# First layer's output projection: the first column pair with a quarter in seven products

## The chip, the cores and the metric

The kernel runs on one core of one Trainium2 chip. The metric is device time in microseconds (us), the median over runs. The profile is of one execution. The engines are TensorE (PE, matmuls, and PEld, its weight loads), VectorE (DVE), ScalarE (ACT), GpSimd (POOL) and SyncE (SP), whose queue issues most loads.

## The reference

A trunk of two layers over 256 tokens and a width of 2048, in float32. The part that matters is the end of the mixer in layer 0:

```
ya = head_rmsnorm(hgrn2(...), a_norm) * silu(za)        # 1024 columns
yb = rg_lru(...) * silu(zb)                             # 1024 columns
y = concatenate([ya, yb])                               # 256 x 2048
h = h + y @ e_w_out                                     # the output projection: 2048 x 2048
pl = rmsnorm(p @ ple_w, ple_norm)
h = h + sigmoid(h @ ple_gate_w) * pl                    # the gate
```

## The kernel before

**Exact products.** Each float32 operand is split into a high part (a cast to float32r) and a low part (the rest). A product is three matmuls: high x high, high x low, low x high. A weight tile of 128x1024 is loaded into the ring `raw` (5 buffers), ACT casts it into `whi`, DVE subtracts into `wlo` (4 buffers each); lines 137 and 138, or 221 and 222 in `split_weights`. An activation tile (tag `ahl`, a ring of 12 in the pool `ap`) holds both parts of 256 inputs for all tokens.

**Quarters.** A projection to 2048 columns has four chunks of 512 columns and four quarters `kq` of 512 inputs. `quarter_tok` (and `plain`, in the other path) loads the two tiles of one quarter of one chunk and does 24 matmuls of 128x128 by 512: two halves of the tokens (`hf`), four blocks of inputs, three matmuls each. `ready(act, lane)` gives `before(kq)`, which drives the lane that makes the activations of that quarter until they are in the program.

**Two chunks as a pair.** `project_two` does chunks 0 and 1 quarter by quarter in the order (0,0) (0,1) (1,0) (1,1) (0,2) (1,2) (0,3) (1,3), into two banks of the PSUM ring `pm` (tag mm) and two of `px` (tag mx).

**Seven products.** `seven` does a pair of chunks with one quarter (kq = 0) by the scheme with seven block products in place of eight. The blocks of the weights are X (chunk 0, side 0), Y (chunk 1, side 1), W (chunk 1, side 0) and Z (chunk 0, side 1); sums of them are formed on DVE (`add`, line 310) and combinations of the activations come from `combos` (tiles q4, two of them, names 1 to 4). Each product is six matmuls of 512 columns (`product`, line 235). Four banks take part: E from `px`, and A, F and B from `pm`. X and Y live in tiles from `room` (tile ch); W and Z come through the ring. `part()` gives two half-tiles, b5 and g (tile pr), which keep products 5 and 6. The string `order` writes out the order by hand: a and b are the next quarter of chunk 0 and 1, digits are products, A and F hand out chunk 0's two halves, a dot lets background lanes advance. At the end E + g (line 318) and B are handed out as chunk 1's halves. `two_and_seven` does the first pair with `project_two` and the second with `seven`, on the combinations that the first pair's time has made. In layer 1's gate (`gates`) the first pair goes through `seven` with the order `LATE` and a quarter of chunk 2 ahead of Y (`third`).

**What is around it.** While the last input projection runs, the inputs y are made: `feature_major` makes y[0] to y[3] and `gated_mix` y[4] to y[7] (line 1048 multiplies by the recurrence's output tt). Each goes tokens to features by DVE transposes (line 699) and a hop through DRAM on POOL's queue (lines 686, 689), 6 steps of the pump after its start. `out_proj` adds each half that is handed out to the residual hq (line 604), transposes it and starts the next hop.

**Pools.** The pool `m0` holds the mixer's tiles (tags f, q, k of two buffers each, and smaller ones); tt lies in tag k. The pool `e0` is opened when m0 is closed and takes the same memory: pr, two tiles ch, gr, wg (set to zero by POOL, line 1141), q4 and row. It serves the second pair of the output projection and the gate. `mixed` closes m0 when the first half of the first pair is handed out:

```
            if (c, hf) == (0, 0):
                m0_scope.close()
                pe0.append(l0.enter_context(tc.tile_pool(name="e0", bufs=1)))
```

The framework orders the instructions of each engine ahead of time, by priorities, and puts in the waits.

Of the kernel before, what the change touches and what calls it, by code (L numbers as in the profile page):

```python
# [19 lines left out]
P = 128  # L20
# [2 lines left out]
KT = D // P  # L23
EPS = 1e-6
RSQRT_MAGIC = 0x5F3759DF
ORDERS = {1: "a5a6.2aA7b.4F.bb", 2: "a5.2aA64.7F.bb"}
LATE = "a526.a7b4aAF.bb"


_PRM = [  # L30
# [15 lines left out]
def trunk(ctx: ExitStack, tc: tile.TileContext, a, out):  # L46
# [113 lines left out]
    def tokens(x, k, hf):  # L160
        return x[:, k, hf * P:(hf + 1) * P]

    def project_tok(w, j, act, before=None, begun=None):

        ps = begun or [pm.tile([P, 512], F32, name="mm", tag="mm") for _ in range(2)]
        for kq in range(1 if begun else 0, 4):
            if before is not None:
                before(kq)
            quarter_tok(w, j, kq, act, ps)
        return ps  # L170
# [13 lines left out]
        for j in range(2, n):  # L184
            yield project_tok(w, j, act)

    def two_and_seven(w, act, before, where, places, home=None, begin=None):

        qs = {}
        start("combos", combos(act, 0, qs, *where))  # L190
        for c, ps in enumerate(project_two(w, act, before)):
            for hf in range(2):
                yield c, hf, ps[hf]
        drain("combos")
        if begin is not None:
            begin()
        for b, hf, src in seven(w, 2, act, qs, (0,), *places(), home and home()):
            yield 2 + b, hf, src
# [42 lines left out]
    def plain(w, j, kq, act, ps, first=(False, False), end=False):  # L241

        parts = load_weights(w[4 * j + kq])
        for hf in range(2):
            product(ps[hf], stationary(act, (2 * kq, 2 * kq + 1), hf), parts, first[hf], end)
            if hf == 0:
                pump()

    def combos(act, kq, qs, pool, tag, bufs=None, offset=0):

        def whole(j):
            x = tp.tile([P, 512], F32, name="xr", tag="hn", bufs=3).rearrange("p (k t) -> p k t", k=2)
            v.tensor_tensor(out=x, in0=act[2 * kq + j][0], in1=act[2 * kq + j][1], op=ALU.add)
            return x[:, :, 0:P], x[:, :, P:T]

        def less(out, x, y):
            with tc.high_priority(offset=offset):
                v.tensor_tensor(out=out, in0=x, in1=y, op=ALU.subtract)

        def pair():  # L260
            c = tp.tile([P, 512], F32, name="qc", tag="th")
            return c, [c[:, i * T:(i + 1) * T].rearrange("p (k t) -> p k t", k=2) for i in range(2)]

        def keep(c, names):
            q = pool.tile([P, 1024], F32R, name="q4", tag=tag, bufs=bufs)
            with tc.high_priority(offset=offset):
                s.copy(q[:, 0:512], c)
                v.tensor_tensor(out=q[:, 512:1024], in0=c, in1=q[:, 0:512].bitcast(F32), op=ALU.subtract)
            for n, name in enumerate(names):
                qs[name, kq] = [[q[:, i * 512 + n * T + k * P:i * 512 + n * T + (k + 1) * P] for k in range(2)]  # L270
                                for i in range(2)]

        while 2 * kq + 1 not in act:
            yield
        a11, a21 = whole(0)
        a12, a22 = whole(1)
        c, (c3, c1) = pair()
        less(c3, a21, a11)
        less(c1, a21, a22)
        keep(c, (3, 1))  # L280
        yield
        d, (c2, c4) = pair()
        less(c2, a11, c1)
        less(c4, a12, c2)
        keep(d, (2, 4))
        yield

    def seven(w, j, act, qs, kqs, room, part, home=None, order=None, acc=None, before=None, third=None):

        def src(b, side, kq):  # L290
            return block(w[4 * (j + b) + kq], side * 1024, 1024)

        def load(tile_of, b, side):
            tiles = []
            for kq in kqs:
                t = tile_of()
                last["sp"] = sy.dma_start(out=t, in_=src(b, side, kq)).ins
                tiles.append(t)
            return tiles

        def ring():
            return wp.tile([P, 1024], F32, name="raw", tag="raw", bufs=5)

        def split(tiles):
            return [split_weights(t) for t in tiles]

        def add(x, y):
            with tc.high_priority(offset=400):
                for xi, yi in zip(x, y):
                    v.tensor_tensor(out=xi, in0=xi, in1=yi, op=ALU.add)  # L310

        def add_loaded(x):
            for xi, kq in zip(x, kqs):
                gp.dma_start(out=xi, in_=src(1, 0, kq), accum_op=ALU.add)

        def soon(out, in0, in1, op):
            with tc.high_priority(offset=450):
                v.tensor_tensor(out=out, in0=in0, in1=in1, op=op)

        def keep(out, bank):  # L320
            with tc.high_priority(offset=450):
                s.copy(out, bank)

        def quadrant(side, hf):
            return stationary(act, [2 * kq + side for kq in kqs], hf)

        def combo(n):
            return [[t for kq in kqs for t in qs[n, kq][x]] for x in range(2)]

        if acc is None:  # L330
            acc = len(kqs) == 2
        rest = [kq for kq in range(4) if kq not in kqs]
        E = px.tile([P, 512], F32, name="mx", tag="mx")
        A, F, B = (pm.tile([P, 512], F32, name="mm", tag="mm") for _ in range(3))
        b5, g = part(), part()
        rows = [list(rest), list(rest)]
        X = load(room, 0, 0)
        product(A, quadrant(0, 0), split(X), True)
        if acc:
            add_loaded(X)  # L340
        with tc.high_priority(offset=450):
            if home is not None:
                with tc.issue_after(last["act"]):
                    s.copy(E, home)
            s.copy(F, A)
            s.activation(B, F, AF.Copy, scale=-1.0)
        if third is not None:
            plain(w, j + 2, kqs[0], act, third, (True, True))
        Y = load(room, 1, 1)
        product(E, combo(4), split(Y), home is None)  # L350
        W = X
        if not acc:
            W = load(ring, 1, 0)
            add(Y, W)
            add(W, X)
        did = set()
        for op in order or ORDERS[len(kqs)]:
            if op in "ab":
                b = "ab".index(op)
                kq = rows[b].pop(0)  # L360
                if before is not None:
                    before(kq)
                plain(w, j + b, kq, act, ((A, F), (E, B))[b], end=not rows[b])
            elif op == "5":
                product(B, combo(1), split(W))
                add(X, Y)
                if acc:
                    add_loaded(Y)
                keep(b5, B)
            elif op == "6":  # L370
                product(B, combo(2), split(X))
                keep(g, B)
            elif op == "2":
                Z = load(ring, 0, 1)
                product(A, quadrant(1, 0), split(Z))
            elif op == "4":
                product(F, quadrant(1, 1), split(X))
            elif op == "7":
                product(B, combo(3), split(Y))
                soon(b5, B, b5, ALU.subtract)  # L380
            elif op == ".":
                pump()
            elif op == "A":
                yield 0, 0, A
            elif op == "F":
                soon(b5, F, b5, ALU.subtract)
                yield 0, 1, b5
            did.add(op)
            if op in "26" and {"2", "6"} <= did:
                add(X, Z)  # L390
        if home is None:
            soon(g, E, g, ALU.add)
            yield 1, 0, g
        else:
            soon(home, E, g, ALU.add)
            yield 1, 0, None
        yield 1, 1, B
# [377 lines left out]
    if True:  # L775
# [311 lines left out]
        for g in range(2):  # L1087
            held[g] = hp.tile([P, 2, 512], F32, name="u", tag="h")
            gate_tok(a["ez"], g, acth, held[g])
            combine()  # L1090
        for g in range(2):
            ps = project_tok(ew, 6 + g, acth)
            u = hp.tile([P, 2, 512], F32, name="u", tag="h")
# [21 lines left out]
        load_hq(i, last["hop"])  # L1115

    def mixed():
        for c, hf, src in two_and_seven(a["eo"], y, ready(y, "fm"), (ap, "ahl"), in_e0):
            if hf == 0 and c in (1, 2):
                load_hq(c + 1, last["hop"])  # L1120
            if (c, hf) == (0, 0):
                m0_scope.close()
                pe0.append(l0.enter_context(tc.tile_pool(name="e0", bufs=1)))
            yield c, hf, src

    def pieces(tile):
        return iter([tile[:, 0:512], tile[:, 512:1024]]).__next__
# [65 lines left out]
    with tc.tile_pool(name="m1", bufs=2) as m1:  # L1193
# [341 lines left out]
        def gates():  # L1535
            third = [pst.tile([P, 512], F32, name="st", tag="st") for _ in range(2)]
            before = ready(act, "fo")
            yield from seven(a["g1"], 0, act, qs1, (0,), *in_m1(), order=LATE, before=before, third=third)
            for hf, ps in enumerate(project_tok(a["g1"], 2, act, None, third)):
                yield 2, hf, ps  # L1540

        for g, hf, src in gates():
# [194 lines left out]
```

## Time and profile before

| | |
|---|---|
| median of 3 runs | 1020.06 us (1020.04 to 1020.19) |
| the profiled execution: time, span | 1020.23 us, 1018.4 us |
| mean granted clock of PE | 0.998 |
| busy: PE, DVE, ACT, POOL | 1009.4, 842.8, 661.4, 101.3 us |
| moved by DMA | 242.66 MB, 238 GB/s on average |
| first pair of the output projection | 300.17 to 343.69 us |
| second pair | 343.69 to 385.85 us |

Times inside the span count from its start. A matmul's row gives about 0.39 us because neighbours overlap in the pipeline; the spacing of starts is what adds up. Lines such as L235 are lines of the kernel before, and a line can be that of a helper.

### The profile page before, as it was taken

Reading aid. Unit: us, or ns where it says so; the run is one execution under the profiler, and the core shown is the slowest. Engines: PE = TensorE matmul, PEld = TensorE weight load, DVE = VectorE, ACT = ScalarE, POOL = GpSimd, SP = SyncE. Lnnn points to the kernel's source line nnn. Section 1 sums busy time; section 2 is a strip of 40 time slices with the busy share of each in tenths; the row PEclk is TensorE's granted clock in tenths of the full one; section 3 lists DMA queues with packets and bytes.
Section 4 is the critical chain, followed back from the end, with each engine's and each line's share of the span. In section 5 each row is a group of like instructions: output and inputs, shape, how many; then the busy total and the mean of one; then the engine's idle time right before and its main releaser. Section 6 shows DMA issues by size and latency. Waiting matters only on the chain.

```text
span 1018.4 us, 14515 instructions
## 1 busy us (share of the span) xinstructions
PE 1009.4 (99%) x5158; PEld 838.1 (82%) x5158; DVE 842.8 (83%) x1234; ACT 661.4 (65%) x949; POOL 101.3 (10%) x182
## 2 busy tenths in 40 slices
PE   9999999999999999999999999999999999999996
PEld 8888888888888888888888888888888888888886
DVE  7858969969687887898669997888889997999794
ACT  7675554686875554666557877776676777466562
POOL 0111101011111112021011100000011110102000
PEclk9999999999999999999999999999999999999999
DMA  9987756567778799487798757567879889696852
GB/s 364 330 233 240 225 177 197 166 204 225 251 235 305 238 315 291 155 284 249 258 337 250 228 166 227 166 208 201 256 193 283 233 249 356 181 288 217 279 186 83
DMA packets 69816, 242.66 MB, mean 238 GB/s; under 512 B 9040, under 2 KB 10448, under 8 KB 69744
## 3 DMA queue, kind: packets, MB, share of 16 engines
q1 hardware_dynamic: 56016, 198.08, 58.7%
q0 software_dynamic: 13296, 43.13, 16.1%
q8 instruction: 40, 0.66, 0.3%
q10 hardware_dynamic: 432, 0.52, 0.1%
q14 instruction: 32, 0.26, 0.1%
HBM read 221.78 MB, written 19.92 MB: 237 GB/s over the span
## 4 chain that ended last, share of the span: by engine, by line
PE 99%; ACT 0%; DMA 0%; issue 0%; DVE 0%; ACTq 0%; POOLq 0%
PE mm L235 29%; PE mm L211 14%; PE mm L212 14%; PE mm L213 14%; PE mx L235 8%; PE mx L211 3%; PE mx L212 3%; PE mx L213 3%; PE mm L517 1%; PE nu L1349 1%; PE mx L517 1%; PE mm L1562 1%; PE mm L1561 1%; PE mm L1563 1%; PE st L213 1%; PE st L235 1%
## 5 line engine op out<-in xcount | busy, mean ns | idle before, releaser
L137 ACT CAST whi<-raw 128x1024 fp32r<-128x1024 f32 (+1 forms) x309 | 322.6, 1047 | 211.3 <-PE mm L213 95.2
L138 DVE TENSOR_TENSOR wlo<-raw,whi 128x1024 fp32r<-128x1024 f32 (+1 forms) x309 | 371.6, 1213 | 104.0 <-ACT whi L137 97.8
L211 PE MATMUL mm<-whi,ahl 128*128 128x512 f32 x640 | 250.5, 392 | 0.0
L212 PE MATMUL mm<-wlo,ahl 128*128 128x512 f32 x640 | 249.4, 390 | 0.0
L213 PE MATMUL mm<-whi,ahl 128*128 128x512 f32 x640 | 249.3, 389 | 0.0
L235 PE MATMUL mm<-whi,ahl 128*128 128x512 f32 x720 | 231.8, 390 | 0.0
L235 PEld LDWEIGHTS mm<-whi,ahl 128*128 128x128 f32 x720 | 135.2, 188 | 27.9
L211 PEld LDWEIGHTS mm<-whi,ahl 128*128 128x128 f32 x640 | 120.2, 188 | 25.5 <-issue 0.4
L213 PEld LDWEIGHTS mm<-whi,ahl 128*128 128x128 f32 x640 | 120.2, 188 | 25.1
L235 PE MATMUL mm<-wlo,ahl 128*128 128x512 f32 x360 | 140.5, 390 | 0.0
L212 PEld LDWEIGHTS mm<-wlo,ahl 128*128 128x128 f32 x640 | 120.2, 188 | 24.3
L222 DVE TENSOR_TENSOR wlo<-ch,whi 128x1024 fp32r<-128x1024 f32 x67 | 81.1, 1221 | 12.5 <-ACT whi L221 11.1
L221 ACT CAST whi<-ch 128x1024 fp32r<-128x1024 f32 x67 | 70.1, 1050 | 26.8 <-PE mm L235 13.8
L235 PEld LDWEIGHTS mm<-wlo,ahl 128*128 128x128 f32 x360 | 67.6, 188 | 14.1 <-DVE wlo L222 0.3
L235 PE MATMUL mx<-whi,ahl 128*128 128x512 f32 x192 | 63.3, 390 | 0.0
L212 PE MATMUL mx<-wlo,ahl 128*128 128x512 f32 x128 | 49.8, 389 | 0.0
L213 PE MATMUL mx<-whi,ahl 128*128 128x512 f32 x128 | 49.8, 389 | 0.0
L211 PE MATMUL mx<-whi,ahl 128*128 128x512 f32 x128 | 49.8, 389 | 0.0
L235 PE MATMUL mm<-whi,q 128*128 128x512 f32 x144 | 49.1, 391 | 0.0
L235 PEld LDWEIGHTS mx<-whi,ahl 128*128 128x128 f32 x192 | 36.1, 188 | 7.9 <-ACT xr L575 0.4
L235 PE MATMUL mx<-wlo,ahl 128*128 128x512 f32 x96 | 37.4, 390 | 0.0
L235 PEld LDWEIGHTS mm<-whi,q 128*128 128x128 f32 x144 | 27.0, 188 | 5.7
(389 smaller groups left out, 1318.5 us busy)
## 6 DMA issues: line engine op xcount, KB each, us to landing
raw<-in_ew_dram SPq DMA_DIRECT2D x64, 512.0 KB, 5.2
raw<-in_g_dram SPq DMA_DIRECT2D x60, 512.0 KB, 4.5
raw<-in_oqk_dram SPq DMA_DIRECT2D x32, 512.0 KB, 5.5
raw<-in_eo_dram SPq DMA_DIRECT2D x30, 512.0 KB, 5.1
raw<-in_oo_dram SPq DMA_DIRECT2D x30, 512.0 KB, 6.4
raw<-in_ov_dram SPq DMA_DIRECT2D x29, 512.0 KB, 4.2
raw<-in_oog_dram SPq DMA_DIRECT2D x24, 512.0 KB, 4.1
raw<-in_oz_dram SPq DMA_DIRECT2D x20, 512.0 KB, 5.1
```

The source lines that it names most:

```text
L137: last["act"] = s.copy(h, r).ins
L138: last["dve"] = v.tensor_tensor(out=l, in0=r, in1=h.bitcast(F32), op=ALU.subtract).ins
L211: te.matmul(ps[hf], xh, wh, start=(k == 0), stop=False, skip_group_check=True)
L212: te.matmul(ps[hf], xh, wl, start=False, stop=False, skip_group_check=True)
L213: last["pe"] = te.matmul(ps[hf], xl, wh, start=False, stop=(k == KT - 1), skip_group_check=True).ins
L221: last["act"] = s.copy(hi, r).ins
L222: last["dve"] = v.tensor_tensor(out=lo, in0=r, in1=hi.bitcast(F32), op=ALU.subtract).ins
L235: last["pe"] = te.matmul(o, x, y, start=(first and k + i == 0), stop=(end and k == n - 1 and i == 2), skip_group_check=True).ins
L517: last["pe"] = te.matmul(ps[hf][:, o:o + w_], tokens(pact[x], k, hf), (hi, lo)[y][:, k * 512 + o:k * 512 + o + w_], start=(n == mine[0]), ...
L1349: te.matmul(ps[:, 0:n], x[:, i, o:o + P], y[:, b, i], start=(b == 0 and x is sh and y is vh), stop=(b == hf and y is vl))
L1561: te.matmul(o, xh, wh, start=(k == 0), stop=False)
L1562: te.matmul(o, xh, wl, start=False, stop=False)
```

## The change

The first pair of the output projection goes through `seven` as well.

- `two_and_seven` gets `first` and `qs`; the first pair then runs `seven(w, 0, ...)` with the order "3a5a6.27ba4AF.bb". Sums of weights are made on DVE, as in the second pair.
- `combos` for it is started ahead of the last two chunks of the input projection, and its two tiles serve both pairs.
- X and Y of the first pair lie in the ring of the activations (tag ahl); b5 and g lie in a tile of m0, in the slots of tag q.
- The bank A of that pair comes from `px`, not `pm`.
- m0 is closed and e0 opened (`in_m0_end`) after the first pair, no longer at its first half.
- In `seven`, Y's product and the sums behind it become the step "3" of the order, and a third chunk's quarter the steps "c" and "d"; the other orders name them so that their sequence stays as it was.
- The function `moved` is new and is not called.

```diff
-ORDERS = {1: "a5a6.2aA7b.4F.bb", 2: "a5.2aA64.7F.bb"}
-LATE = "a526.a7b4aAF.bb"
+ORDERS = {1: "3a5a6.2aA7b.4F.bb", 2: "3a5.2aA64.7F.bb"}
+LATE = "c3a526.a7b4aAF.bb"
...
-    def two_and_seven(w, act, before, where, places, home=None, begin=None):
-
-        qs = {}
-        start("combos", combos(act, 0, qs, *where))
-        for c, ps in enumerate(project_two(w, act, before)):
-            for hf in range(2):
-                yield c, hf, ps[hf]
+    def two_and_seven(w, act, before, where, places, home=None, begin=None, first=None, qs=None):
+
+        if first is not None:
+            drain("combos")
+            yield from seven(w, 0, act, qs, (0,), *first(), order="3a5a6.27ba4AF.bb", before=before, first=px)
+        else:
+            qs = {}
+            start("combos", combos(act, 0, qs, *where))
+            for c, ps in enumerate(project_two(w, act, before)):
+                for hf in range(2):
+                    yield c, hf, ps[hf]
         drain("combos")
         if begin is not None:
             begin()
...
-        A, F, B = (pm.tile([P, 512], F32, name="mm", tag="mm") for _ in range(3))
+        A, F, B = (p.tile([P, 512], F32, name=n, tag=n)
+                   for p, n in ((first, "mm" if first is pm else "mx"), (pm, "mm"), (pm, "mm")))
...
-        if third is not None:
-            plain(w, j + 2, kqs[0], act, third, (True, True))
-        Y = load(room, 1, 1)
-        product(E, combo(4), split(Y), home is None)
-        W = X
-        if not acc:
-            W = load(ring, 1, 0)
-            add(Y, W)
-            add(W, X)
...
+            if op in "cd":
+                plain(w, j + 2, "cd".index(op), act, third, (op == "c",) * 2)
+            elif op == "3":
+                Y = load(room, 1, 1)
+                product(E, combo(4), split(Y), home is None)
+                W = X
+                if not acc:
+                    W = load(ring, 1, 0)
+                    add(Y, W)
+                    add(W, X)
...
+        qsy = {}
+        start("combos", combos(y, 0, qsy, ap, "ahl"))
         for g in range(2):
             ps = project_tok(ew, 6 + g, acth)
...
-        for c, hf, src in two_and_seven(a["eo"], y, ready(y, "fm"), (ap, "ahl"), in_e0):
+        for c, hf, src in two_and_seven(a["eo"], y, ready(y, "fm"), None, in_e0, None, in_m0_end, in_m0, qsy):
             if hf == 0 and c in (1, 2):
                 load_hq(c + 1, last["hop"])
-            if (c, hf) == (0, 0):
-                m0_scope.close()
-                pe0.append(l0.enter_context(tc.tile_pool(name="e0", bufs=1)))
             yield c, hf, src
+
+    def in_m0():
+        return (lambda: ap.tile([P, 1024], F32, name="ch", tag="ahl"),
+                pieces(m0.tile([P, 1536], F32, name="pr", tag="q")[:, 0:1024]))
+
+    def in_m0_end():
+        m0_scope.close()
+        pe0.append(l0.enter_context(tc.tile_pool(name="e0", bufs=1)))
```

More of the change, by code (lines that the diff above doesn't have):

```diff
@@ L161, in tokens, with project_tok @@
         return x[:, k, hf * P:(hf + 1) * P]
-    def project_tok(w, j, act, before=None, begun=None):
+    def project_tok(w, j, act, before=None, begun=None, done=0):
         ps = begun or [pm.tile([P, 512], F32, name="mm", tag="mm") for _ in range(2)]
-        for kq in range(1 if begun else 0, 4):
+        for kq in range(done, 4):
             if before is not None:
@@ L247, in plain, with moved, known @@
                 pump()
+    def moved(qs, kq, pool, tag):
+        for q, names in qs["tiles", kq]:
+            t = pool.tile([P, 1024], F32R, name="q4", tag=tag)
+            s.copy(t, q.bitcast(F32))
+            known(qs, kq, t, names)
+            yield
+    def known(qs, kq, q, names):
+        for n, name in enumerate(names):
+            qs[name, kq] = [[q[:, i * 512 + n * T + k * P:i * 512 + n * T + (k + 1) * P] for k in range(2)]
+                            for i in range(2)]
     def combos(act, kq, qs, pool, tag, bufs=None, offset=0):
@@ L268, in keep @@
                 v.tensor_tensor(out=q[:, 512:1024], in0=c, in1=q[:, 0:512].bitcast(F32), op=ALU.subtract)
-            for n, name in enumerate(names):
-                qs[name, kq] = [[q[:, i * 512 + n * T + k * P:i * 512 + n * T + (k + 1) * P] for k in range(2)]
-                                for i in range(2)]
+            known(qs, kq, q, names)
+            qs.setdefault(("tiles", kq), []).append((q, names))
         while 2 * kq + 1 not in act:
@@ L286, in combos, with seven @@
         yield
-    def seven(w, j, act, qs, kqs, room, part, home=None, order=None, acc=None, before=None, third=None):
+    def seven(w, j, act, qs, kqs, room, part, home=None, order=None, acc=None, before=None, third=None, first=pm):
         def src(b, side, kq):
@@ L346, in seven @@
             s.activation(B, F, AF.Copy, scale=-1.0)
-        if third is not None:
-            plain(w, j + 2, kqs[0], act, third, (True, True))
-        Y = load(room, 1, 1)
-        product(E, combo(4), split(Y), home is None)
-        W = X
-        if not acc:
-            W = load(ring, 1, 0)
-            add(Y, W)
-            add(W, X)
         did = set()
         for op in order or ORDERS[len(kqs)]:
-            if op in "ab":
+            if op in "cd":
[8 more added lines that the diff above has]
+                    add(W, X)
+            elif op in "ab":
                 b = "ab".index(op)
@@ L1538, in gates @@
             yield from seven(a["g1"], 0, act, qs1, (0,), *in_m1(), order=LATE, before=before, third=third)
-            for hf, ps in enumerate(project_tok(a["g1"], 2, act, None, third)):
+            for hf, ps in enumerate(project_tok(a["g1"], 2, act, None, third, 1)):
                 yield 2, hf, ps
```

## The prediction

> **What bounds the kernel now.** I read the page's busy time first, then its chain, then TensorE's waits, then the stretches that the change touches.
>
> ```profile
> PE 1009.4 (99%) x5158; PEld 838.1 (82%) x5158; DVE 842.8 (83%) x1234; ACT 661.4 (65%) x949; POOL 101.3 (10%) x182
> PE 99%; ACT 0%; DMA 0%; issue 0%; DVE 0%; ACTq 0%; POOLq 0%
> ```
>
> TensorE (PE) is busy all the time, and the chain that ended last is all PE. The view of PE's waits has one row:
>
> ```profile
> PE st L99 <- PEq L1728: 0.8, 1, 0.8
> ```
>
> That wait is at the start, so between the first and the last matmul PE waits for nothing. A matmul taken away is worth its spacing; a wait put anywhere into PE's stream is lost in full. Now the two column pairs of the first output projection, by the windows view and the chain in order of time:
>
> ```profile
> 300.17:343.69 43.52, 43.52 (x194) 36.05 (x193) 32.66 (x40) 21.26 (x24) 5.25 (x9) 1.00 0.76 258
> 343.69:385.85 42.16, 42.16 (x188) 34.92 (x187) 37.16 (x46) 24.01 (x31) 8.98 (x16) 1.00 0.91 301
> ...
> 343.69 1.36 PE mm L235 x6
> 345.06 1.36 PE mx L235 x6
> ```
>
> Columns: length, then busy time (instructions) of PE, weight loads, DVE, ACT, POOL, and the clock, 1.00. Pair one now takes eight quarters of 24 matmuls (192) in 43.52 us; pair two is already of the changed form, 7 products of 6 and 6 quarters of 24 (186), in 42.16 us. A product is six matmuls and 1.36 us; each matmul costs 0.227 us.
>
> **The change, step by step.**
>
> *Matmuls.* Pair one gets pair two's count: 192 - 186 = 6 fewer, 43.52 - 42.16 = 1.36 us gained, so it would end at 342.33. This is 0.13% of the kernel, and nothing else in the change can give more.
>
> *DVE and ACT.* 19 weight splits instead of 16, four sums of 128x1024, three corrections of 128x512; the combinations move ahead.
>
> ```profile
> L138 DVE TENSOR_TENSOR wlo<-raw,whi 128x1024 fp32r<-128x1024 f32 x14 | 17.1, 1221 | 9.5 <-ACT whi L137 9.0
> L310 DVE TENSOR_TENSOR raw<-raw,ch 128x1024 f32<-128x1024 f32 x1 | 1.2, 1210 | 0.0
> L318 DVE TENSOR_TENSOR pr<-mm,pr 128x512 f32<-128x512 f32 x2 | 1.4, 684 | 0.0
> ...
> 263.10 0.69 DVE L152 TENSOR_TENSOR ahl<-xr,ahl 128x512 fp32r<-128x512 f32 x1 [0.37 <-ACT ahl L151]
> 268.37 2.36 DVE L138 TENSOR_TENSOR wlo<-raw,whi 128x1024 fp32r<-128x1024 f32 x2 [4.58 <-ACT whi L137]
> 297.00 1.29 DVE L253 TENSOR_TENSOR xr<-ahl 128x512 f32<-128x512 f32 x2
> 313.74 0.69 DVE L268 TENSOR_TENSOR q<-qc,q 128x512 fp32r<-128x512 f32 x1
> ```
>
> DVE gains 3 x 1.22 + 4 x 1.21 + 3 x 0.68 = 10.5 us here and ACT three casts. The combinations (now from 297.00 to 314.4) can run as soon as y's first two tiles are there, at 263.8, where DVE next idles 4.58 us; their q is then ready long before the second product asks at 301.5. Pair two does the same set of work within 37.16 us of DVE in its 42.16, and PE never waits there. I cost it at nothing; the cover is DVE's remaining 5 us.
>
> *Order of y.* The new order reaches quarter 2 after three products and one quarter: 300.17 + 3 x 1.36 + 5.44 = 309.7 (its second tile 1.36 later, 311.1), and quarter 3 after six products and three quarters, at 324.7. Before they were due four and six quarters in, 321.9 and 332.8. From the timelines of DVE and POOL and the view of the tile dzb:
>
> ```profile
> 306.52 0.68 DVE L1048 TENSOR_TENSOR xr<-r,tt 128x512 f32<-128x512 f32 x1
> 312.00 0.68 DVE L152 TENSOR_TENSOR ahl<-xr,ahl 128x512 fp32r<-128x512 f32 x1
> 324.20 1.29 DVE L1048 TENSOR_TENSOR xr<-r,tt 128x512 f32<-128x512 f32 x2
> 325.58 1.29 DVE L152 TENSOR_TENSOR ahl<-xr,ahl 128x512 fp32r<-128x512 f32 x2
> ...
> 287.09 2.18 POOL L689 DMA_DIRECT2D r<-dzb  x4 [4.16 <-ACT xr L717]
> 309.15 2.18 POOL L689 DMA_DIRECT2D r<-dzb  x4 [3.99 <-DMA dzb<-w]
> DMA to landing us min/median/max: 4.2/5.5/7.4
> ```
>
> With the old times quarter 2's second tile is ready at 312.7, 1.6 us late, and quarter 3's at 326.9, 0.8 us after its own due time (324.7 + 1.36). Both can move up: the transposed data are in after the fourth issue, 289.3 and 311.3, plus about 5.5 us. DVE loses the combinations from this stretch, so I take 0; the ends are 0 and 1.6 us.
>
> *Pair one's chain tiles and banks.* X and Y take slots of the activations' ring that the last input projection frees every 5.44 us, so X is loaded by about 295; A lies in the other PSUM ring and needs no bank of that projection. The same 16 loads of 512 KB go through SP's queue. Nothing.
>
> *The pool.* This step decides. The two half-tiles b5 and g now lie in a tile of m0 (`in_m0`), so m0 closes only after pair one has been handed out, and e0 opens after that. e0 holds X and Y of pair **two**.
>
> ```profile
> 287.15 2.29 DVE L1038 TENSOR_TENSOR_SCAN tt<-av,it 128x1024 f32<-128x1024 f32 x1
> 325.56 0.81 SPq L297 DMA_DIRECT2D ch<-in_eo_dram  x2
> 325.61 0.52 POOL L1141 MEMSET wg<- 128x512 f32 x1 [12.85 <-ACT ahl L151]
> SPq L297 <- DVE xr L1048: 0.9, 1, 0.9
> ```
>
> (Timelines of DVE, SP and POOL, and SP's waits.) Both e0 tiles, X's load on SP and wg's memset on POOL, start within 0.1 us of the end of the last L1048 (324.20 + 1.29 = 325.49), the last instruction that reads a tile of m0 (tt). SP's own waits name it. By the sizes in the code X lies where m0 kept f and later av, which the scan at 287.15 was the last to touch; so I read that the hold is for the whole pool, not for the overlapping tile. It costs nothing before: 18 us remain until X's product at 343.69. After the change the last reader of m0 is the addition of g to hq, behind pair one's last quarter. Pair two shows how long that takes, and the view of the tile ch what a load into it and its split take:
>
> ```profile
> 383.28 0.68 DVE L318 TENSOR_TENSOR pr<-mx,pr 128x512 f32<-128x512 f32 x1
> 383.88 0.68 DVE L253 TENSOR_TENSOR xr<-ahl 128x512 f32<-128x512 f32 x1
> 384.48 0.69 DVE L604 TENSOR_TENSOR hq<-pr,hq 128x512 f32<-128x512 f32 x1
> ...
> DMA to landing us min/median/max: 4.4/5.2/6.0
> 336.93 1.05 ACT L221 CAST whi<-ch 128x1024 fp32r<-128x1024 f32 x1 [2.71 <-PE mm L213]
> 338.01 1.23 DVE L222 TENSOR_TENSOR wlo<-ch,whi 128x1024 fp32r<-128x1024 f32 x1 [1.00 <-ACT whi L221]
> ```
>
> E is complete 12 matmuls before the pair's end (385.85 - 2.72 = 383.13) and g is read by 385.17, 2.04 us later. In the changed pair one: 342.33 - 2.72 + 2.04 = 341.65, and X is issued 0.07 later, at 341.72. The two loads into ch landed after 4.4 and 6.0 us; I take X 4.4 (346.12) and Y, issued 0.43 later, 6.0 (348.15). Cast and split end 2.31 after the cast's start: X's low part at 348.5, Y's at 350.5. The second of six matmuls needs the low part, so Y's product ends 5 x 0.227 later, at 351.6, against 342.33 + 2.72 = 345.05 without a wait: 6.6 us lost. The ends of this term: no operation between the two on DVE (0.6 us less) and 3.4 us for both landings, the least that the loads into raw took, give 4.3; one more split of 1.22 ahead of the addition and 1.6 us more per landing give 9.4. The view of the tile raw, from 310 to 350:
>
> ```profile
> DMA to landing us min/median/max: 3.4/4.9/8.5
> ```
>
> Behind X on SP wait Y and later raw loads; the first raw tiles of pair two go ahead as slots are free. On POOL the memset, 0.52 us, waits too; the hop of columns 0 would lie before it. Nothing later absorbs the loss, since PE has no other slack.
>
> The Trainium skill (DMA: Bandwidth & Descriptors, section Anatomy of one DMA) fits a transfer on the gpsimd path as 2.0 us plus the bytes at 436 GB/s, as an estimate 3.2 us for 512 KB; with that for both landings the term would be 4.7 us and the total 1.9 us lower. The rows above, 4.4 and 6.0 on SP, are longer, so the sum does not go by it.
>
> *The clock.* PE would stand from 342.5 to X's first matmul at 347.2, 4.7 us. What a pause does is seen only at the kernel's end:
>
> ```profile
> 1010.04 0.28 PE L1563 MATMUL mm<-whi,ahl 128*128 128x256 f32 x1
> 1013.00:1014.00 1.00, 0.00 (x0) 0.00 (x0) 1.00 (x4) 0.72 (x1) 0.00 (x0) 0.69 0.00 0
> ...
> 0.78 3.75 PE L99 MATMUL st<-const-float32-1.0 128*128 128x128 f32 x16 [0.78 <-PEq L1728]
> 4.18 3.40 PE L517 MATMUL mx<-whi,ahl 128*128 128x256 f32 x12
> 7.42 1.08 PE L517 MATMUL mx<-wlo,ahl 128*128 128x512 f32 x4
> ```
>
> PE ends at 1010.32; the slice from 1013 to 1014 has a granted clock of 0.69, which is half clock for its last 0.62 us, from 1013.38, 3.06 us after. So 4.7 us is enough. At the start PE works from 0.78 and is at full pace by 7.42 at the latest: at most 6.6 us at half pace, 3.3 us lost. The other end is 0. I take 1.0: with 3.06 us for the way back as well, seven matmuls are slow, 1.6 us, of which part lies under Y's wait. The Trainium skill (TensorE: Matmul & The Clock Gate, Part 1) puts both transitions at a free-running window of about 3.4 us; by it a pause of 4.7 us may or may not hold a whole idle window, which is the second rival.
>
> *Sum* against the profiled execution (1020.23 us, span 1018.4): 1020.23 - 1.36 + 6.6 + 1.0 = 1026.5. The median is 0.17 lower: 1026.3.
>
> **Rivals.**
> 1. *Not slower: the gain alone.* X's load is not held by g, because the edge is for a narrower region than the whole pool and neither chain tile shares g's bytes. For it: before, one load only shows the rule. Against: X and wg start together, on two queues. It decides if X is issued before 342.33 - 4.4 - 2.4 = 335.5. Then 1020.06 - 1.36 = 1018.7.
> 2. *The hold, with the clock kept.* 4.7 us may fall across two windows. 1020.06 - 1.36 + 6.6 = 1025.3.
> 3. *y late, no hold:* quarter 2 waits its 1.6 us: 1020.3. On top of the forecast: 1027.9.
>
> **How the numbers follow.** Forecast, hold with half clock: 0.47; rival 2: 0.35; rival 1: 0.13; rival 3 alone: 0.03; a larger gain by something unseen: 0.02. The range holds the first two with most of their ends: 1022.6 (4.3 instead of 6.6, no clock loss, is 1023.0; a little below) to 1030.6 (9.4 and 1.0 give 1029.1; 6.6 and 3.3 with 1.6 for y give 1030.2). Some 0.8 lies in it. A measurement tells 0.2%, about 2 us, from no change: faster 0.02, same 0.15 (rivals 1 and 3), slower 0.83.
>
> **What would show it.** Right: 186 matmuls in pair one; the loads into ch on SP just after the addition into hq that reads g, the memset beside them; a row of PE's waits at L235 of some 5 us or more near 342, from the split of ch; a clock under 1.00 there. Wrong: those loads before 335, or PE without a wait at the pair's end. A wait of PE at 309 to 313 would be y; one in the middle of the pair on wlo would be DVE's cover gone.

## The result, and the profile after

The changed kernel takes 1036.41 us (median of four runs, 1035.65 to 1037.54) against 1020.12 for the kernel before on the same chip (1020.04 to 1020.27): slower by a ratio of 1.016, 95% interval 1.0144 to 1.0176. The forecast was 1026.3 with a range of 1022.6 to 1030.6. Its sign was right; the time lies 5.8 us above the range.

The profiled execution took 1036.12 us with a span of 1034.3, 15.9 more than before. First the page's busy line and its chain by engine:

```profile
PE 1015.0 (98%) x5152; PEld 839.2 (81%) x5152; DVE 853.2 (82%) x1244; ACT 664.8 (64%) x956; POOL 101.3 (10%) x182
PE 91%; DMA 4%; ACT 2%; DVE 1%; issue 1%; POOL 0%; ACTq 0%; DVEq 0%; POOLq 0%
```

TensorE issues six matmuls fewer (5152 against 5158), as the change intends, but the chain is no longer all PE: loads, ACT and DVE stand in it now. Next the waits of PE, changed kernel (waiting line, what released it: us in total, times, longest). Most lines below the diff have moved: split_weights is now L225 and L226, `product` L239, `add` L327, E + g L335, the copies into the banks F and B L363 and L364, the addition into hq L623, the loads L314.

```profile
PE mm L239 <- ACT whi L225: 4.8, 1, 4.8
PE mx L239 <- ACT mm L363: 3.3, 1, 3.3
...
PE mx L239 <- DVE wlo L226: 0.6, 1, 0.6
PE mm L239 <- DVE wlo L226: 0.5, 1, 0.5
PE st L1180 <- DMA r<-dfg: 0.4, 1, 0.4
```

Matmul starts divide the time between the pairs (timeline of PE, changed kernel): the first matmul of pair one, the last one before its longest wait, the first of the last twelve of pair one (bank B), and the first behind pair two.

```profile
300.30 0.39 PE L239 MATMUL mx<-whi,ahl 128*128 128x512 f32 x1
...
303.68 0.40 PE L239 MATMUL mx<-whi,q 128*128 128x512 f32 x1
...
347.30 0.39 PE L239 MATMUL mm<-whi,ahl 128*128 128x512 f32 x1
...
400.60 0.39 PE L215 MATMUL mm<-whi,ahl 128*128 128x512 f32 x1
```

Twelve matmuls are 2.72 us, so pair one ends at 350.02 and took 49.72 us; pair two took 50.58. The form with seven products takes 42.16 when PE never waits. **Lost: 7.56 us in pair one and 8.42 in pair two.** With the 1.36 gained that is 14.6 of the 15.9. Of the other 1.3 the wait of 0.4 us in the gate (L1180) and one of 0.3 behind it (L239, on a split) are a part; the rest was not followed up.

**Pair two: the held load.** The chain of waits around the boundary, changed kernel, in order of time, and the row of SP's own waits:

```profile
347.50 0.70 DVE pr L335
...
348.22 0.70 DVE hq L623
...
348.94 4.81 DMA ch<-in_eo_dram
...
353.85 1.05 ACT whi L225
...
354.93 1.24 DVE wlo L226
...
356.21 2.50 PE mm L239 x5
358.71 2.59 PE mx L239 x6
```

```profile
SPq L314 <- DVE hq L623: 6.5, 1, 6.5
```

This is the predicted chain, link for link: E + g, the addition into hq that reads g, X's load 0.02 us behind it, cast, split, product. PE waits 4.77 us for X's cast and 0.47 for its low part. The last eleven matmuls take 5.09 us where eleven spacings are 2.49. The clock is at half there, but it is not what sets most of that time. Y's load landed only 7.3 us after its issue (view of the tile ch), so Y's low part comes late (timelines of DVE and PE, changed kernel):

```profile
357.78 1.23 DVE L226 TENSOR_TENSOR wlo<-ch,whi 128x1024 fp32r<-128x1024 f32 x1 [1.63 <-ACT whi L225]
...
359.06 0.79 PE L239 MATMUL mx<-wlo,q 128*128 128x512 f32 x1
```

The second matmul of Y's product starts as that split ends (359.01). Five spacings at full clock would have ended the product at 360.2, which is 7.5 us later than the 352.74 of a pair two without a wait. Only the remaining 0.9 us of the 8.42 are half clock.

**Pair one: the first two tiles come late.** Timelines of SP and then of ACT, changed kernel:

```profile
287.16 1.46 SPq L134 DMA_DIRECT2D raw<-in_eo_dram  x2
288.67 1.27 SPq L314 DMA_DIRECT2D ch<-in_eo_dram  x2
...
297.60 1.05 ACT L225 CAST whi<-ch 128x1024 fp32r<-128x1024 f32 x1 [6.29 <-DMA ch<-in_eo_dram]
300.11 1.05 ACT L225 CAST whi<-ch 128x1024 fp32r<-128x1024 f32 x1 [1.47 <-DMA ch<-in_eo_dram]
301.49 0.62 ACT L151 CAST ahl<-xr 128x512 fp32r<-128x512 f32 x1 [0.33 <-DVE xr L1067]
302.13 1.28 ACT L1118 ACT_TABLE_LOAD   x1
...
306.09 0.69 ACT L1119 ACTIVATE u<-mm,rcr 128x512 f32<-128x512 f32 x1
306.66 0.61 ACT L363 COPY mm<-mx 128x512 f32<-128x512 f32 x1
```

X and Y are issued at 288.67, as the third and fourth load of 512 KB within 2.8 us. The DMA view from 285 to 302 has the median landing (the last number, us) of these loads, of the other weight loads and of the four reads of y[4]'s hop, first after, then before:

```profile
raw<-in_eo_dram SPq DMA_DIRECT2D x4, 512.0 KB, 6.6
ch<-in_eo_dram SPq DMA_DIRECT2D x2, 512.0 KB, 9.6
...
r<-dzb POOLq DMA_DIRECT2D x4, 128.0 KB, 8.7
```

```profile
raw<-in_eo_dram SPq DMA_DIRECT2D x7, 512.0 KB, 4.7
```

The hop slowed down as well: its four reads took 6.8 us before (same view). How much of the late landings comes from the loads issued together and how much from the hop beside them was not tried.

ACT works in a fixed order. X's and Y's casts stand in it ahead of what takes the last input projection out of its banks (the evacuations, L1118 and L1119) and ahead of the copy of A into F (L363). While ACT waits for Y it does none of these, though the projection's first half was complete at about 297.6 (300.30 less twelve spacings). Between Y's cast and the evacuations stands the cast of y[4] (L151), whose hop landed at 300.64. In the kernel before, the evacuations began 6.3 us earlier and y[4]'s cast came behind them, at 307.24 (timeline of ACT, before):

```profile
295.85 1.28 ACT L1097 ACT_TABLE_LOAD   x1
```

F is ready at 307.27. PE, done with Y's product at 304.08, can start chunk 0's next quarter, which adds into A, only at 307.33, and runs at half clock until 313.

### The profile page after: what moved, and what is told of

Same layout as the page of the kernel before. It is cut to its first block, busy times and chain, and to the rows that moved or that the text cites. A ratio compares the mean times of both kernels' runs of the same rounds, so it can differ in the third digit from the quotient of the medians.

```text
span 1034.3 us, 14520 instructions
## 1 busy us (share of the span) xinstructions
PE 1015.0 (98%) x5152; PEld 839.2 (81%) x5152; DVE 853.2 (82%) x1244; ACT 664.8 (64%) x956; POOL 101.3 (10%) x182
## 4 chain that ended last, share of the span: by engine, by line
PE 91%; DMA 4%; ACT 2%; DVE 1%; issue 1%; POOL 0%; ACTq 0%; DVEq 0%; POOLq 0%
PE mm L239 28%; PE mm L215 13%; PE mm L216 13%; PE mm L217 13%; PE mx L239 10%; PE mx L215 2%; PE mx L217 2%; PE mx L216 2%; PE mm L536 1%; DMA r<-dfg 1%; DMA r<-dzb 1%; PE nu L1375 1%; PE mx L536 1%; PE mm L1588 1%; PE mm L1589 1%
## 5 line engine op out<-in xcount | busy, mean ns | idle before, releaser
L138 DVE TENSOR_TENSOR wlo<-raw,whi 128x1024 fp32r<-128x1024 f32 (+1 forms) x305 | 366.1, 1212 | 93.0 <-ACT whi L137 87.7
L137 ACT CAST whi<-raw 128x1024 fp32r<-128x1024 f32 (+1 forms) x305 | 317.8, 1046 | 192.0 <-PE mm L217 87.9
L239 PE MATMUL mm<-whi,ahl 128*128 128x512 f32 x772 | 249.8, 391 | 4.8 <-ACT whi L225 4.8
L239 PEld LDWEIGHTS mm<-whi,ahl 128*128 128x128 f32 x772 | 145.6, 189 | 35.2 <-ACT whi L225 5.2
L239 PE MATMUL mm<-wlo,ahl 128*128 128x512 f32 x386 | 151.0, 391 | 0.5 <-DVE wlo L226 0.5
L225 ACT CAST whi<-ch 128x1024 fp32r<-128x1024 f32 x72 | 75.2, 1050 | 47.9 <-DMA ch<-in_eo_dram 23.0
L226 DVE TENSOR_TENSOR wlo<-ch,whi 128x1024 fp32r<-128x1024 f32 x72 | 87.2, 1221 | 22.6 <-ACT whi L225 21.1
L239 PE MATMUL mx<-whi,ahl 128*128 128x512 f32 x248 | 83.8, 399 | 3.3 <-ACT mm L363 3.3
L239 PEld LDWEIGHTS mm<-wlo,ahl 128*128 128x128 f32 x386 | 72.8, 189 | 16.0 <-DVE wlo L226 1.0
L239 PEld LDWEIGHTS mx<-whi,ahl 128*128 128x128 f32 x248 | 47.6, 192 | 14.1 <-ACT mm L363 3.7
L239 PE MATMUL mm<-whi,q 128*128 128x512 f32 x156 | 53.3, 390 | 0.0
L239 PE MATMUL mx<-wlo,ahl 128*128 128x512 f32 x124 | 49.6, 400 | 0.3 <-DVE wlo L138 0.3
L215 PE MATMUL mx<-whi,ahl 128*128 128x512 f32 x96 | 37.4, 389 | 0.0
L217 PE MATMUL mx<-whi,ahl 128*128 128x512 f32 x96 | 37.4, 389 | 0.0
L239 PEld LDWEIGHTS mm<-whi,q 128*128 128x128 f32 x156 | 29.3, 188 | 6.2
```

The source lines that it names most:

```text
L137: last["act"] = s.copy(h, r).ins
L138: last["dve"] = v.tensor_tensor(out=l, in0=r, in1=h.bitcast(F32), op=ALU.subtract).ins
L215: te.matmul(ps[hf], xh, wh, start=(k == 0), stop=False, skip_group_check=True)
L217: last["pe"] = te.matmul(ps[hf], xl, wh, start=False, stop=(k == KT - 1), skip_group_check=True).ins
L225: last["act"] = s.copy(hi, r).ins
L226: last["dve"] = v.tensor_tensor(out=lo, in0=r, in1=hi.bitcast(F32), op=ALU.subtract).ins
```

## The experiments

The table gives, for each profiled execution, the loss against 42.16 us in each pair, worked out from the starts of pair one, of its last twelve matmuls and of the next stage as above. All but the last row are versions of the changed kernel; ratios are against the kernel before on the same chip. A profile shows one execution: those of early, fix3 and fix4 have the lowest time of their version (1029.15, 1021.80, 1020.23 us) and that of ring the highest (1024.78), so versions are compared by their medians.

| | pair one, us | pair two, us | median us | ratio, 95% interval |
|---|---|---|---|---|
| changed | 7.56 | 8.42 | 1036.41 | 1.016 (1.0144 to 1.0176) |
| hold | 14.40 | 1.77 | 1034.99 | 1.0148 (1.0132 to 1.0163) |
| hold2 | 8.21 | 1.76 | 1029.91 | 1.0089 (1.0072 to 1.0106) |
| early | 1.59 | 8.76 | 1030.04 | 1.0102 (1.0085 to 1.0119) |
| order | 8.06 | 8.45 | 1034.76 | 1.0155 (1.0131 to 1.0178) |
| fix | 10.71 | 1.77 | 1030.85 | 1.0105 (1.009 to 1.012) |
| fix2 | 2.67 | 1.76 | 1023.52 | 1.0031 (1.0019 to 1.0043) |
| fix3 | 1.70 | 1.76 | 1023.48 | 1.0032 (1.002 to 1.0043) |
| fix4 | 1.99 | 0.00 | 1020.91 | 1.0012 (1.0003 to 1.0021) |
| ring | 4.08 | 0.00 | 1021.40 | 1.0011 (1.0002 to 1.0019) |
| combos (before, one part) | | | 1020.28 | 1.0006 (0.9997 to 1.0016) |

**hold: the pool's hold taken away.** b5 and g go into the ring h, so nothing of m0 is needed through pair one, and m0 is closed at the first half that is handed out, as before.

```diff
-        for ... in two_and_seven(a["eo"], y, ready(y, "fm"), None, in_e0, None, in_m0_end, in_m0, qsy):
+        for ... in two_and_seven(a["eo"], y, ready(y, "fm"), None, in_e0, None, None, in_m0, qsy):
...
+            if (c, hf) == (0, 0):
+                in_m0_end()
...
-                pieces(m0.tile([P, 1536], F32, name="pr", tag="q")[:, 0:1024]))
+                pieces(hp.tile([P, 1024], F32, name="pr", tag="h")))
```

> The half-tiles b5 and g go into a tile of the h ring, so that m0 closes at the first half again; nothing else differs from the changed kernel. In the trace of the changed kernel pair one ends at 349.95 and E's product of pair two at 361.07, where 352.67 would be without a wait: 8.4 us. Theory of the held pool: X and Y of pair two load before 340, PE has no wait there, 1036.4 - 8.4 = 1028.0. Rival (the load is late for another reason, the DMA queues or SP's order): the wait stays, 1034 to 1036.

1034.99 us: almost nothing came back. But the hold itself is gone. SP loads X of pair two at 329.55, and pair two's loss falls from 8.42 to 1.77. PE's waits and the timelines of SP and ACT, version hold:

```profile
PE mm L239 <- ACT pr L339: 4.4, 2, 2.8
```

```profile
329.55 0.80 SPq L314 DMA_DIRECT2D ch<-in_eo_dram  x2
...
328.95 1.22 ACT L151 CAST ahl<-xr 128x512 fp32r<-128x512 f32 x2 [4.13 <-DVE xr L1067]
330.08 0.58 ACT L339 COPY pr<-mm 128x512 f32<-128x512 f32 x1
```

A new loss took its place in pair one: the copies of products 5 and 6 into b5 and g (L339) come late on ACT, the second one behind the casts of y's last two tiles, for which ACT waited 4.13 us. By the time alone the rival would have looked right; the three starts show two opposite changes. That the ring h is what put these copies late is tried next.

**hold2: the same with another home for b5 and g,** the ring wt of the pool bp.

```diff
-                pieces(hp.tile([P, 1024], F32, name="pr", tag="h")))
+                pieces(bp.tile([P, 1024], F32, name="pr", tag="wt")))
```

> As the run hold, but b5 and g lie in a tile of bp's ring wt, which is free when they are first written; in hold they waited in the h ring for the last projection's u, and PE stood 4.4 us on their copies. Theory of the held pool: the 8.4 us at pair two's start go, 1028.0; with the 1.5 us that hold showed on bank B at product 5, 1029.5. Rival (what the hold cost is paid again in another wait, whatever place b5 and g have): 1033 to 1036.

1029.91: 6.5 us below the changed kernel. No wait on L339 is left, so their home it was; why the framework orders the copies later with the ring h was not tried further. Pair two loses 1.76, by a wait that the hold had covered (PE's waits and the timeline of DVE, version hold2):

```profile
PE mm L239 <- ACT mm L364: 1.5, 1, 1.5
```

```profile
356.17 0.68 DVE L623 TENSOR_TENSOR hq<-mm,hq 128x512 f32<-128x512 f32 x1
```

Product 5 of pair two needs the copy into its bank B (L364), that bank is pair one's B, and DVE adds pair one's B into hq only at 356.17, behind splits and sums for pair two.

**early: X and Y of pair one loaded early.** They go into the slots of m0's tag q, free long before, and b5 and g into another tile of m0; the hold stays.

```diff
-        return (lambda: ap.tile([P, 1024], F32, name="ch", tag="ahl"),
-                pieces(m0.tile([P, 1536], F32, name="pr", tag="q")[:, 0:1024]))
+        return (lambda: m0.tile([P, 1536], F32, name="ch", tag="q")[:, 0:1024],
+                pieces(m0.tile([P, 1024], F32, name="pr", tag="A", bufs=1)))
```

> X and Y of pair one go into m0's two q slots, free since 272, in place of the activations' ring; b5 and g into m0's tile A; m0 still closes after the pair. In the changed kernel pair one takes 49.65 us in place of 42.16, 7.5 more. Theory of Y's late landing (issued at 288.67 after a wait for a slot of the ring, landed at 300.1; ACT stands in front of its cast, with the projection's last evacuations and the copy of A to F behind it): the loads are issued before 280, the wait of 3.3 us and the half clock behind it go, the wait at pair two stays: 1036.4 - 7.5 = 1028.9. Rival, y[4]'s cast (its data landed at 300.64) is what stands in ACT's queue: little changes, 1034 to 1036. Rival, DVE's added sums: 1036.

1030.04: 6.4 us below the changed kernel. PE's waits and the timeline of SP, version early:

```profile
PE mm L239 <- ACT whi L225: 5.3, 1, 5.3
PE mx L239 <- DVE wlo L138: 1.1, 1, 1.1
```

```profile
272.50 0.33 SPq L314 DMA_DIRECT2D ch<-in_eo_dram  x1
```

X's load starts 16 us earlier, the wait on the copy into F is gone, pair one's loss falls to 1.59, and pair two keeps its 8.76. With the two loads out of the way, the hop of y[4] is faster too (DMA view from 285 to 302, version early):

```profile
r<-dzb POOLq DMA_DIRECT2D x4, 128.0 KB, 4.9
```

**order: the casts of y[4] and y[5] put behind the projection's last evacuation on ACT** (`evac[0]` in the diff). This tells whether ACT stood for y rather than for the weights.

```diff
-                y[4 + 2 * j + b] = split_act(x, "y")
+                with tc.issue_after(evac[0]):
+                    y[4 + 2 * j + b] = split_act(x, "y")
```

> The changed kernel with one edge more: the casts of y[4] and y[5] on ACT stay behind the last evacuation of the input projection; only their place in ACT's order differs. Theory of Y's late landing: Y's cast still ends at 301.2, the copy of A to F comes only 1.0 us earlier (0.62 for the cast, 0.33 for its wait), with some of the half clock: 1034 to 1036. Rival, y[4]'s cast is the blocker: the wait of 3.3 us and its half clock go, about 1030.

1034.76, an interval that overlaps the changed kernel's, and pair one still loses 8.06 us; PE still waits for the copy into F (PE's waits, version order):

```profile
PE mx L239 <- ACT mm L363: 2.5, 1, 2.5
PE mx L239 <- DVE wlo L138: 1.5, 1, 1.5
```

So the late weights are enough to hold ACT: with y's cast out of the way, Y's cast (at 299.78) still stands ahead of the evacuations, and the copy into F comes only 0.9 us earlier against pair one's start. That does not clear y. In the changed kernel y[4]'s hop landed 0.6 us behind Y, and early brought both forward. The run ring below shows that a late y[4] can do the same by itself.

**fix and fix2: both causes removed.** fix is early's X and Y with b5 and g in the ring h and m0 closed as in hold; fix2 has b5 and g in the ring wt instead.

> Both at once: X and Y of pair one in m0's q slots, b5 and g in the h ring, m0 closed at the first half. Both theories right: 1036.4 - 8.4 - 7.5 = 1020.5, and with no wait left the six matmuls' 1.36 us below the kernel before, 1018.7. If one of the two is wrong: 1028 to 1029. If DVE's added work or y's earlier due times have a price of their own, it shows here as waits of PE inside pair one: 1020 to 1023.

> As fix, with b5 and g in wt's ring. If fix missed its 1020.5 because of its copies' place (5.9 us of waits on them, and half clock behind one of them): 1036.4 - 8.4 - 7.5 + 1.5 for bank B = 1022.0. If y[6] and y[7], whose hop starts 5 us later than before the change, are what stands in front of the copies: PE still waits at product 6 or at quarter 3, 1028 to 1031.

fix came to 1030.85, with hold's trouble again (`PE mm L239 <- ACT pr L339` 5.9 us). fix2 came to 1023.52. The two gains measured singly were 6.5 and 6.4: 1036.4 - 12.9 = 1023.5. **By the medians the two losses are independent and add up.** fix2 differs from hold2 in nothing but the place of X and Y, so the 6.4 us between these two (1029.91 - 1023.52) are theirs alone. What is left are small waits of PE: 1.5 us on the copy into bank B, 1.2 on a split and 0.3 on the copy into F.

**fix3: the transposes of the last projection's output raised to the priority of the splits.**

```diff
+        with tc.high_priority(offset=450 if name == "dzb1" else 0):
             for hf in range(2):
                 v.transpose(w5[:, hf], ...)
```

> As fix2, with the two transposes of the last projection (the start of the hop for y[6] and y[7]) given the splits' priority, so that DVE no longer does three splits and a sum ahead of them. If that hop is on PE's path in fix2, this takes its wait away: 1 to 6 us below fix2. If not: within 0.5 us of fix2, or slower by what the two transposes delay the splits, up to 1.3.

1023.48, no gain: the hop of y[6] and y[7] starts 4.6 us earlier (its write at 306.17, fix2's at 310.72), but PE was not waiting for it.

**fix4: the addition of pair one's bank B (L623) raised ahead of the splits.**

```diff
-                with tc.high_priority(offset=100):
+                with tc.high_priority(offset=450 if lane == "fe" and c == 1 and hf else 100):
                     v.tensor_tensor(out=hq[c][:, hf], in0=src, in1=hq[c][:, hf], op=ALU.add)
```

> fix3, and the addition of pair one's bank B into hq gets a priority of 450, so that DVE does it ahead of the last five splits and sums of pair two's start (it was started 349.10, behind them). TensorE's one wait of 1.47 us on the copy B<-F at 350.5 should go, since DVE reaches the addition about 4.5 us earlier. Theory (the bank is the last wait of the second pair): fix3's 1023.5 less 1.5 and less some clock, 1021.5 to 1022.0, with one wait left (0.7 on the low part of a split at 305). Rival (a product's start is limited by DVE's amount of work, not by its order): the wait moves to a split pushed behind the addition, and the time stays at 1023.0 or above.

1020.91, 0.6 us below what was expected: pair two now loses nothing. PE's waits, then the timeline of DVE, then a row of the windows view (length, then busy us (instructions) of PE, weight loads, DVE, ACT and POOL; then the clock, the DMA share and GB/s), version fix4:

```profile
PE mx L239 <- DVE wlo L138: 0.7, 1, 0.7
PE mx L239 <- ACT mm L363: 0.3, 1, 0.3
```

```profile
344.79 0.68 DVE L623 TENSOR_TENSOR hq<-mm,hq 128x512 f32<-128x512 f32 x1
```

```profile
298.00:306.00 8.00, 7.01 (x29) 4.99 (x28) 8.00 (x10) 7.99 (x12) 0.00 (x0) 1.00 0.19 65
```

Even so it does not beat the kernel before (ratio 1.0012, 1.0003 to 1.0021). Pair one still loses 1.99 us, more than the 1.36 that six matmuls are worth. The last row says where it is lost: from 298 to 306, at the passage from the input projection to pair one, DVE and ACT are busy without a gap. Just ahead of this stretch both wait for y[4]: DVE stands 0.86 us until its hop has landed at 295.96, ACT 1.49 us until its cast at 296.81 (their timelines). Whether the amount of work or this landing sets the time was not tried.

**ring: bank A of pair one back in pm,** on top of fix4.

```diff
-                 order="3a5a6.27ba4AF.bb", before=before, first=px)
+                 order="3a5a6.27ba4AF.bb", before=before)
```

> fix4 with that part of the change undone that puts pair one's bank A into the ring px; A comes from pm. By the ring of three buffers A then takes the bank that the projection's chunk before last left, F and B those of its last chunk. Theory (the prediction's: the bank's ring is worth nothing): the copies into F and B stand behind the last evacuations on ACT anyhow (they end at 302.4 to 303.1), so the time is fix4's within 0.5. Rival: F or B waits for a bank: a new wait of TensorE of 1 to 3 us between 302 and 308, and 1 to 5 us over fix4.

1021.40, within 0.5 of fix4, with overlapping intervals: in the runs the ring of A is worth nothing that can be told. The profiled execution, which took the longest of this version, does show a wait of PE where the rival had one, 1.68 us on the copy into F. It comes from y[4] and not from a bank (timeline of ACT, version ring):

```profile
300.73 0.62 ACT L151 CAST ahl<-xr 128x512 fp32r<-128x512 f32 x1 [2.91 <-DVE xr L1068]
```

X and Y had been cast by 297.82. ACT then stood 2.91 us for y[4], whose hop took 7.2 us to land (5.7 in fix4), and went on from its cast to the evacuations and the copy into F (at 305.91) without a gap. So y[4], late by itself, also holds the evacuations. A version with X and Y early and y[4]'s cast behind the evacuations was not run.

**combos: the kernel before with the combinations started early, and nothing else.**

> The kernel before with one part of the change: the combinations are started ahead of the last two chunks of the input projection; pair one stays with its eight quarters. The prediction's step (they lie in DVE's idle time and cost nothing): 1020.1, within 0.3. Rival, they delay the hop for y[4] (in the changed kernel it starts 2.3 us later): since before the change y[4] is due 12 us later, still 1020.1; if it costs something by DVE's or ACT's order, 1021 to 1023.

1020.28 against 1020.08: no difference, and PE waits nowhere from 295 to 440. That part of the change costs nothing.

## Why the prediction was wrong in size

- **Matmuls, -1.36.** Right: 5152 against 5158 on the page, and pair two of fix4, undisturbed, takes 42.16 again.
- **The pool, +6.6, and the clock, +1.0.** The mechanism is shown, by the chain and by hold and hold2. X was issued 1.08 us before pair one's end (0.61 forecast) and landed in 4.81 us (4.4 forecast); PE's wait for X was 4.77 (4.7 forecast). Together 8.42 instead of 7.6. The undersized part is the landing of Y, 7.3 us instead of 6.0: the hold costs 7.5, and the clock 0.9 on top of it (1.0 forecast). Taking the hold away returned 6.5, since the wait for bank B then takes 1.5 back. The memset of wg, told as a sign, did not stand beside the loads: it came at 352.53, behind a hop on POOL's queue.
- **"X is loaded by about 295 ... Nothing."** This is the step that failed. Slots of the ring were indeed free by then (X was issued at 288.67), but the step gave no landing for X or Y among the loads issued beside them: X was there at 297.6, Y at 300.1. And it left out what stands behind their casts on ACT: the evacuations and the copy into F. Its price was put at 0; it is most of the 7.56 us lost in pair one, of which early gives 6.0 back.
- **DVE and ACT, "nothing; the cover is DVE's remaining 5 us".** The amount was right (DVE 853.2 against 842.8 us, 10.4 more; 10.5 forecast) and moving the combinations cost nothing, but the cover was wrong, by a size that the larger waits hid. An average over 42 us is no cover for the eight in which the projection's end and pair one's beginning meet: 1.7 to 2.0 us in fix3 and fix4, part of which may be y[4]'s, and bank B's 1.76 in pair two.
- **Order of y, 0.** Not a wait of PE in the changed kernel at 309 to 313, and none in fix4. But the step looked at PE alone. In the changed kernel y[4]'s cast stands ahead of the evacuations on ACT, and its hop landed at 300.64, 9.3 us after its fourth issue (291.32), where about 5.5 was taken. Why the framework put that cast there was not tried; combos, where it stays behind them, rules out the early combinations alone. Y's late landing hid this; in ring's profiled execution it is a wait by itself, and in hold and fix ACT stood 4.13 and 5.54 us for y's last two tiles.
- **The rivals.** The one with the clock kept is refuted (half clock from 354.04 to 360.86), though it cost only 0.9; the gain alone is refuted too. None had a loss at pair one's beginning, and so the range could not hold the time: with 7.56 there the sum would have been 1033.9, and with 8.42 for the pool 1034.7.

## What to carry to other kernels

When a step moves a load into another ring, follow it to its landing among the loads issued beside it, and then to the in-order engine that casts it: what is queued behind the cast waits too, and that was here the evacuation of the stage before. The same holds for any cast that comes to stand ahead of those evacuations, as y[4]'s did here. A step that costs "nothing" by an engine's mean share over a stage should be checked in the few microseconds where two stages meet. And where a fix seems to do nothing, split its time by stages before dropping it: hold removed 6.7 us in one pair and added 6.8 in the other.

## What the runs showed of the hardware

A short wait of PE can cost as much again in clock. The windows view of the changed kernel in slices of 1 us (columns as above; the granted clock is the third number from the right):

```profile
306.00:307.00 1.00, 0.00 (x0) 0.00 (x0) 1.00 (x3) 1.00 (x3) 0.00 (x0) 0.62 0.00 0
...
313.00:314.00 1.00, 1.00 (x6) 0.80 (x5) 1.00 (x2) 0.00 (x0) 0.00 (x0) 0.96 1.05 311
...
354.00:355.00 1.00, 0.05 (x1) 0.06 (x1) 0.07 (x1) 0.89 (x1) 0.00 (x0) 0.52 0.96 226
...
360.00:361.00 1.00, 1.00 (x4) 0.75 (x3) 1.00 (x2) 0.71 (x2) 1.00 (x2) 0.57 0.00 0
```

A slice at 0.62 is half clock for 0.76 us of it, so the first spell runs from 306.24 to 313.08 and the second from 354.04 to 360.86: 6.84 and 6.82 us, though PE was back at work 1.1 and 0.9 us after their start. The spells begin 47.80 us apart. The timeline of PE and the same windows view of version ring, around its wait of 1.68 us:

```profile
304.50 0.39 PE L239 MATMUL mx<-whi,q 128*128 128x512 f32 x1
306.57 0.51 PE L239 MATMUL mm<-whi,ahl 128*128 128x512 f32 x1 [1.68 <-ACT mm L363]
```

```profile
307.00:308.00 1.00, 0.98 (x3) 0.75 (x3) 1.00 (x3) 1.00 (x3) 0.00 (x0) 0.61 0.00 0
...
310.00:311.00 1.00, 1.00 (x4) 0.76 (x4) 1.00 (x1) 0.40 (x1) 0.56 (x1) 0.69 0.59 119
```

Here half clock runs from 307.22 to 310.62, 3.40 us, and begins after PE had resumed. The Trainium skill (TensorE: Matmul & The Clock Gate, Part 1) describes a free-running window of 3413 ns. These traces agree with such a grid: spells of one and of two windows, and 47.80 us are 14.0 of them. They do not agree with the table that the Trainium skill has there, by which the clock falls after an idle window. The waits of 3.25 us before 307.33 and of 1.68 us before 306.57 are both shorter than a window; in the 3.41 us before 306.24 PE had worked 1.24 us, and in those before 307.22 about 1.7. Waits of 1.47 us (bank B in fix2) and 1.62 us (the first of the two on L339 in hold) left the clock at 1.00. With the time from 296 to 400 us laid out in such steps of 3.41 us, in the traces of all versions, every fall follows a step with at most 1.7 us of work, and no step with 1.9 us or more is followed by one. So here every wait from 1.68 us up brought one or two windows at half pace. What PE loses by it after its return is half of what is left of the spell: 2.9 us in pair one of the changed kernel (307.33 to 313.08) and 1.7 in ring. In pair two, the only place for which the prediction had allowed for it (1.0), Y's late load hid all but 0.9.
